# Strassen–Winograd down projection of a hybrid diffusion layer: its block products in another order, the last one's resident blocks loaded during the four products ahead of it, and the final norm by half rows

## The chip, the cores and the metric

The kernel runs on one core of one Trainium2 chip. The metric is the device time of one execution of the whole layer in microseconds (us), the median of several runs. Nothing is shared with other cores; all waits are between the engines of this core (TensorE, VectorE, ScalarE, GpSimd, and SyncE, which here only issues DMAs) and its DMA queues.

## The reference, cut to what matters

One layer over 1024 tokens of width D = 1024: a mixer (delta-rule and state-space heads) with a gated residual, then a gated MLP with a depthwise 3x3 convolution, another gated residual and a final RMS norm. The change lies in the last two lines only:

```python
def conv_glu(h, w_gate, w_up, conv_w, conv_b, w_down, on_grid):
    a = h @ w_gate
    ...
    return (jax.nn.silu(a) * (h @ w_up)) @ w_down
...
        x = x + g2 * conv_glu(modulate(rmsnorm(x, norm2_g[l]), sh2, sc2), *ffn_params, True)
        ...
    return rmsnorm(x, final_norm_g)
```

with `w_down` 2816 x 1024 (D_FF = 2816) and `rmsnorm(x, g) = x * rsqrt(mean(x*x) + EPS) * g`.

## The kernel before, in words

**The down projection as seven products.** The gated activations A (2816 features x 1024 tokens) and the weights B = `w_down` are cut into halves both ways, and the product is made by Winograd's form of Strassen's scheme with seven products instead of eight: P1 = A11·B11, P2 = A12·B21, P3 = S4·B22, P4 = A22·T4, P5 = S1·T1, P6 = S2·T2, P7 = S3·T3. The S are sums of quarters of A, the T of quarters of B. While gate and up are computed, GpSimd's queue writes all of A's seven operands to DRAM (`sa_d`) and the four T (`sw_d`); B11, B21 and B22 are read from `w_down` itself.

**One product.** The shared dimension is 1408 = NP x 128 with NP = 11, so a product is 11 blocks. A block has a stationary side (128 features x 512 tokens) and a moving side (128 features x 512 columns). `block()` fetches each side: a DMA of SyncE's queue into a raw buffer (`ra` or `rb`, two buffers each, L1418), a cast to fp32r on ScalarE (`sh`, `vh`: the high part, L1419) and a subtraction on VectorE (`sl`, `vl`: what the cast lost; it is issued through the helper of L95). These four have three buffers each, handed out by `parts()`. `mul()` (L1433) then runs three matmuls for one of the four token tiles of 128: high x high, high x low, low x high. A block is thus 12 matmuls on four PSUM banks, one bank a token tile, and a product 132. `accA` and `accB` are two sets of four banks; two successive products use different sets, so that the sums of one can be read while the next one runs.

**What is made of the products.** With s1 = P1, s2 = P1 + P6 and s3 = s2 + P7 (SBUF tiles `sn0`, `sn1`, `sn2` of four token tiles each), the four quarters of the result are P1 + P2 (token tiles 0 to 3, low columns `LOH`), s2 + P5 + P3 (tiles 0 to 3, high columns `HIH`), s3 + P5 (tiles 4 to 7, `HIH`) and s3 - P4 (tiles 4 to 7, `LOH`). `put(t, q, src)` multiplies a 128 x 512 piece by the gate row `g2row` into a temporary (`tm`, three buffers) and adds it to `x1[t]`, the residual stream of tile t in SBUF (`x_0` to `x_7` in the listings): two VectorE instructions. `put` is linear, so a quarter may be put in pieces: s2 + P5 and P3 are put one after the other.

**The order before** is P1 P6 P2 P7 P5 P4 P3. The last product has its first HEAD = 3 blocks like all others; the other eight (NLC = 8) are loaded into the space of the MLP's input `mxs`, which is free by then (`mxh`, `mxl`: high and low parts). They are called the resident blocks. With all of them in SBUF the matmuls can be run token tile by token tile instead of block by block. `final()` is the RMS norm of a whole row: ScalarE squares with a running sum, VectorE scales, GpSimd takes the power -1/2 (L1289), and one VectorE instruction (`stt`, L107) multiplies by that and by the gain row into `ot`, from where two DMAs write the row's halves, one issued by SyncE, one by ScalarE. For the very last tile the squares and the last multiply go by halves.

**What sets the order of the instructions.** The code is written product by product, but a scheduler orders the instructions of all engines by its own times ahead of the run, within their dependences. Each engine and each DMA queue then works through its list in order: what stands at the head and waits holds up all that is behind it. So the code's order is not the order on the engines, and the listings below are of the latter.

Of the kernel before, what the change touches and what calls it, by code (L numbers as in the profile page):

```python
# [13 lines left out]
ALU = mybir.AluOpType  # L14
# [59 lines left out]
def hybrid_layer(ctx: ExitStack, tc: tile.TileContext, x, c, cx, c_ctx, w_ada, b_ada, norm1_g, w_in,  # L74
# [13 lines left out]
    def T(pool, shape, name, dt=F32, **kw):  # L88
        return pool.tile(list(shape), dt, name=name, **kw)
# [1307 lines left out]
    accA = accB = None  # L1397


    PRODS = ("P1", "P6", "P2", "P7", "P5", "P4", "P3")  # L1400
    STA = dict(P1=0, P2=1, P4=2, P3=3, P5=4, P6=5, P7=6)
    MOV = dict(P5=0, P6=1, P7=2, P4=3)
    WD = dict(P1=(0, 0), P2=(1, 0), P3=(1, 1))
# [25 lines left out]
    def mul(pb, t, ops, start, stop):  # L1429
        (sh, sl), (vh, vl) = ops  # L1430
        tk = slice(t * P, (t + 1) * P)
        for n, (a, w) in enumerate(((sh, vh), (sh, vl), (sl, vh))):
            nc.tensor.matmul(pb, a[:, tk], w, start=start and n == 0, stop=stop and n == 2)  # L1433

    def product(p, acc, js, first, last):
        for j in js:
            ops = block(p, j, *parts())
            for t in range(4):
                mul(acc[t], t, ops, first and j == js[0], last and j == js[-1])

    with pool("fp") as fp:
        for n_, b_ in (("wr", 3), ("wh", 3), ("wl", 3)):
# [95 lines left out]
    with pool("p3") as p3:  # L1538
        s1, s2, s3 = (T(p3, [P, 4, 512], f"sn{i}") for i in range(3))
        g2 = rows[3]  # L1540
        accB = [bank(b) for b in ("A", "B", "E", "tp")]
        LOH, HIH = slice(0, 512), slice(512, D)

        def tmp_():
            cnt[0] += 1
            return T(p3, [P, 512], f"tm{cnt[0]}", tag="tm", bufs=3)

        def put(t, q, src):
            m = tmp_()
# [4 lines left out]
        def final(t, last):
            if "f" not in rows:
                rows["f"] = T(p3, [P, D], "gfrow")
                nc.sync.dma_start(rows["f"], final_norm_g.partition_broadcast(P))
            jk = T(p3, [P, D], f"fj{t}", tag="fj", bufs=2)
            ot = T(p3, [P, D], f"ot{t}", tag="ot", bufs=3)
            halves = [slice(0, 512), slice(512, D)]  # L1560
            if not last:
                rs = rstd_tok(x1[t], jk, t, 1)
                stt(ot, x1[t], rs, rows["f"], ALU.mult, ALU.mult)
            else:
                rs, a = ss2[:, 1, t:t + 1], ss2[:, 0, 0:2]
                for c, q in enumerate(halves):
                    act(jk[:, q], x1[t][:, q], AF.Square, accum_out=a[:, c:c + 1])
                tt(rs, a[:, 0:1], a[:, 1:2], ALU.add)
                ts(rs, rs, 1.0 / D, ALU.mult, EPS, ALU.add)
                nc.gpsimd.tensor_tensor(rs, rs, mhalf[:, 0:1], op=ALU.pow)  # L1570
            for c, q in enumerate(halves):
                if last:
                    stt(ot[:, q], x1[t][:, q], rs, rows["f"][:, q], ALU.mult, ALU.mult)
                (nc.scalar if c else nc.sync).dma_start(out[t * P:(t + 1) * P, q], ot[:, q])

        allj = range(NP)
        product("P6", accB, range(NP - 1), True, False)
        product("P1", accA, [NP - 1], False, True)
        for t in range(4):
            nc.scalar.copy(s1[:, t, :], accA[t])  # L1580
        product("P6", accB, [NP - 1], False, True)
        for t in range(4):
            tt(s2[:, t, :], accB[t], s1[:, t, :], ALU.add)
        product("P2", accA, allj, True, True)
        for t in range(4):
            m = tmp_()
# [20 lines left out]
        ops = []
        for u in range(NLC):
            sta, mov = ([m[:, u, 4 * i:4 * i + 4, :].rearrange("p k c -> p (k c)") for m in mxs] for i in range(2))
            ops.append(block("P3", HEAD + u, sta, mov))  # L1610
# [38 lines left out]
```

## Time and profile before

| | |
|---|---|
| median of 3 runs | 1557.68 us (1556.49 to 1559.80) |
| profiled execution | 1551.18 us |
| its span, first to last instruction | 1549.5 us |
| TensorE busy | 1450.4 us, 94% |
| VectorE busy | 1099.1 us, 71% |
| ScalarE busy | 694.1 us, 45% |
| GpSimd busy | 513.9 us, 33% |
| granted TensorE clock, mean | 0.974 |
| DMA traffic | 266.72 MB, 172 GB/s over the span |

The profile is of one execution, which is why it has a time of its own; its span leaves out what lies before the first and behind the last instruction. Times in it are us from the start of the span. Where an instruction is listed with its start, the next figure is its duration, then come engine, line, operation, output<-inputs and shape, and in square brackets how long its engine had been idle before and what ended that. The line of most VectorE instructions is that of a helper (L95 for a two-tensor operation, L102 for one with constants, L107 for a three-operand one), and L92 is ScalarE's, so that the tiles' names tell them apart. The seven products take up the last 245 us or so of the span.

### The profile page before, as it was taken

What the parts mean: (1) busy time and instruction counts of PE and PEld (TensorE: products, weight loads), DVE (VectorE), ACT (ScalarE), POOL (GpSimd) and SP (SyncE); (2) the same over time, 40 slices, a digit from 0 to 9 for tenths busy, and PEclk for the clock granted to TensorE, in tenths of its full rate; (3) what the DMA queues carried; (4) which work ended last, traced back from release to release, by engine and by line L of the source; (5) the groups of instructions that cost most, each with busy time, mean ns of one, the idle gap of its engine ahead of it and who ended that gap; (6) DMA issues with size and microseconds to landing.
All of it is one profiled execution on the core that took longest, in us unless ns stands there. A gap on an engine that the chain in (4) does not pass through costs nothing.

```text
span 1549.5 us, 23952 instructions
## 1 busy us (share of the span) xinstructions
PE 1450.4 (94%) x8344; PEld 1211.5 (78%) x8344; DVE 1099.1 (71%) x1749; ACT 694.1 (45%) x1552; POOL 513.9 (33%) x645
## 2 busy tenths in 40 slices
PE   5899988899999899998989799999999999999996
PEld 2577767778888789997767688888888888888885
DVE  6877688978535666547976887777778776456597
ACT  6566655636666656454243422222222221344444
POOL 3654499782226785201472111101111111000002
PEclk9999999999999999999999899999999999999998
DMA  8354877654668675535851434334444432566665
GB/s 279 120 160 136 234 224 215 166 149 120 177 192 292 207 263 168 150 117 179 291 169 69 149 120 146 125 133 156 143 149 156 144 140 105 180 198 194 191 188 192
DMA packets 255416, 266.72 MB, mean 172 GB/s; under 512 B 50657, under 2 KB 193630, under 8 KB 255296
## 3 DMA queue, kind: packets, MB, share of 16 engines
q1 hardware_dynamic: 238815, 212.90, 45.1%
q0 software_dynamic: 15136, 49.55, 8.4%
q10 hardware_dynamic: 1344, 2.75, 0.5%
q8 instruction: 66, 1.08, 0.3%
q14 instruction: 55, 0.44, 0.1%
HBM read 191.87 MB, written 73.27 MB: 171 GB/s over the span
## 4 chain that ended last, share of the span: by engine, by line
PE 60%; DVE 10%; DMA 8%; POOL 7%; issue 6%; ACT 2%; SPq 1%; POOLq 0%; DVEq 0%; ACTq 0%
PE bk L1298 29%; PE bk L1433 10%; PE bk L619 6%; PE bk L453 5%; POOL Zs L98 2%; POOL pr L98 2%; DMA rb<-rows_d 1%; PE bk L1346 1%; DMA owr<-in_w_out_dram 1%; DVE rs L107 1%; DVE fac L107 1%; DMA R<-rows_d 1%; PE bk L997 1%; DVE owl L95 1%; PE bk L1005 1%
## 5 line engine op out<-in xcount | busy, mean ns | idle before, releaser
L1298 PE MATMUL bk<-mxh,fh 128*128 128x512 f32 x672 | 262.5, 391 | 8.4 <-DVE fac L95 8.4
L1298 PE MATMUL bk<-mxl,fh 128*128 128x512 f32 x672 | 262.5, 391 | 0.0
L1298 PE MATMUL bk<-mxh,fl 128*128 128x512 f32 x672 | 262.0, 391 | 0.2 <-DVE fl L95 0.2
L107 DVE SCALAR_TENSOR_TENSOR fac<-gpad,v,fac 128x1024 f32<-128x1024 f32 x176 | 224.9, 1281 | 4.9 <-ACT fac L92 2.0
L1298 PEld LDWEIGHTS bk<-mxh,fh 128*128 128x128 f32 x672 | 126.8, 189 | 35.0 <-DVE fac L95 8.8
L1298 PEld LDWEIGHTS bk<-mxh,fl 128*128 128x128 f32 x672 | 126.7, 189 | 27.2 <-DVE fl L95 0.7
L1298 PEld LDWEIGHTS bk<-mxl,fh 128*128 128x128 f32 x672 | 126.7, 189 | 26.3
L1456 ACT CAST fh<-fr 128x1024 fp32r<-128x1024 f32 x42 | 44.3, 1055 | 228.9 <-PE bk L1298 215.6
L1520 POOL DMA_DIRECT2D sa_d<-fac x44 | 23.7, 540 | 352.0 <-issue 214.1
L453 PE MATMUL bk<-hh,wh 128*128 128x512 f32 x320 | 129.6, 406 | 0.8 <-DVE v L254 0.7
L453 PE MATMUL bk<-hh,wl 128*128 128x512 f32 x320 | 129.1, 403 | 0.0
L453 PE MATMUL bk<-hl,wh 128*128 128x512 f32 x320 | 128.1, 400 | 0.0
L95 DVE TENSOR_TENSOR fl<-fr,fh 128x1024 fp32r<-128x1024 f32 x42 | 51.3, 1221 | 101.6 <-ACT fh L1456 91.5
L1433 PE MATMUL bk<-vl,sh 128*128 128x512 f32 x276 | 107.5, 389 | 0.0
L1433 PE MATMUL bk<-vh,sl 128*128 128x512 f32 x276 | 107.4, 389 | 0.0
L1419 ACT CAST sh<-ra 128x512 fp32r<-128x512 f32 x69 | 43.0, 624 | 119.5 <-PE bk L1433 99.1
L95 DVE TENSOR_TENSOR sl<-ra,sh 128x512 fp32r<-128x512 f32 x69 | 47.5, 689 | 63.8 <-ACT sh L1419 63.8
L1289 POOL TENSOR_TENSOR ss<-ss,mhalf 128x1 f32<-128x1 f32 x15 | 13.9, 931 | 221.9 <-DVE ss L104 221.9
L1433 PE MATMUL bk<-vh,sh 128*128 128x512 f32 x276 | 75.7, 389 | 0.0
L453 PEld LDWEIGHTS bk<-hh,wh 128*128 128x128 f32 x320 | 61.7, 193 | 13.5 <-PE bk L252 0.9
L453 PEld LDWEIGHTS bk<-hh,wl 128*128 128x128 f32 x320 | 61.4, 192 | 13.1 <-issue 0.9
L453 PEld LDWEIGHTS bk<-hl,wh 128*128 128x128 f32 x320 | 61.7, 193 | 11.9 <-DVE hl L95 0.2
(386 smaller groups left out, 3730.7 us busy)
## 6 DMA issues: line engine op xcount, KB each, us to landing
ra<-sa_d SPq DMA_DIRECT2D x77, 256.0 KB
kv<-kv_d SPq DMA_DIRECT2D x80, 192.0 KB
yq<-yq_d SPq DMA_DIRECT2D x64, 192.0 KB
awa<-in_w_ada_dram SPq DMA_DIRECT2D x24, 512.0 KB
fr<-in_ffn_w_up_dram SPq DMA_DIRECT2D x22, 512.0 KB
dr<-in_ffn_w_down_dram SPq DMA_DIRECT2D x22, 512.0 KB
sa_d<-fac POOLq DMA_DIRECT2D x44, 256.0 KB, 2.3
rb<-sw_d SPq DMA_DIRECT2D x44, 256.0 KB
```

The lines of the kernel that those rows point to most:

```text
L95: nc.vector.tensor_tensor(o, a, b, op=op)
L98: nc.gpsimd.tensor_tensor(o, a, b, op=op)
L107: nc.vector.scalar_tensor_tensor(o, a, s, b, op0=op0, op1=op1)
L453: paced(nc.tensor.matmul(pb[:, :bn], w[i][:, kk, :], hview(h, k, b0, bn), start=(n == 0), stop=(n == 3 * KT - 1)))
L619: mm = nc.tensor.matmul(pb[:, 256 * j:256 * j + 256], m[:, k, tk], w, start=(n == 0), stop=(n == 3 * KT - 1))
L997: mm = nc.tensor.matmul(hi[d], yq[:, 0, :], r, start=True, stop=True)
L1005: mm = nc.tensor.matmul(lo[d], kd, ns[d], start=True, stop=True)
L1298: nc.tensor.matmul(pv, w(k), h[:, b4, k, :], start=(n == 0), stop=(n == 3 * KT - 1))
L1419: nc.scalar.copy(th, raw)
L1433: nc.tensor.matmul(pb, a[:, tk], w, start=start and n == 0, stop=stop and n == 2)
L1456: hi["last"] = nc.scalar.copy(wh, raw)
L1520: nc.gpsimd.dma_start(sa_d[i][j], t)
```

## The change

The order of the products becomes P1 P6 P7 P5 P4 P3 P2. What goes with it:

- **The last product is P2.** Its eight resident blocks are no longer loaded behind its own first three, but one by one through a hook that `product()` calls behind a block (`ahead`): one in P7, two in P5, three in P4, two in P3. They stay in `mxs` until the end.
- **The pieces are put at other times.** P1's part of the low columns of tiles 0 to 3 goes in on its own, in the code behind P7 (on VectorE the scheduler places it behind the end of P6), and P2's part at the end. s2 + P5 is put behind P4 in the code instead of behind P5.
- **The final norm goes by half rows.** The gain row is fetched before the first of the last products and scaled by sqrt(D) on ScalarE. `half1` handles the half of a row that is complete first: square with its sum on ScalarE, D·EPS added to the sum, the half multiplied by the gain in place. `half2` handles the other half: square, sum of the two halves' sums, power on GpSimd, the last multiply of this half on VectorE and of the other half on ScalarE (a copy with a scale). Both halves are written to the output from `x1` itself (L1580 by SyncE, L1581 by ScalarE); the tiles `ot` are gone. Before, this was for the last tile only, and both multiplies were VectorE's.

The number of products, blocks and matmuls is as before. The core of the diff:

```diff
-    PRODS = ("P1", "P6", "P2", "P7", "P5", "P4", "P3")
+    PRODS = ("P1", "P6", "P7", "P5", "P4", "P3", "P2")
...
-    def product(p, acc, js, first, last):
+    def product(p, acc, js, first, last, between=None):
         for j in js:
             ops = block(p, j, *parts())
             for t in range(4):
                 mul(acc[t], t, ops, first and j == js[0], last and j == js[-1])
+            if between is not None:
+                between(j)
...
+        gf = rows["f"] = T(p3, [P, D], "gfrow")
+        nc.sync.dma_start(gf, final_norm_g.partition_broadcast(P))
+        nc.scalar.mul(gf, gf, float(D) ** 0.5)
+        sq = T(p3, [P, 2, NLC], "sq")
...
+        def half1(t, q, c):
...
+            square(t, 0, q)
+            ts(sq[:, 0, t:t + 1], sq[:, 0, t:t + 1], D * EPS, ALU.add)
+            tt(x1[t][:, q], x1[t][:, q], gf[:, q], ALU.mult)
+
+        def half2(t, q, c):
+            square(t, 1, q)
+            rs = ss2[:, 1, t:t + 1]
+            tt(rs, sq[:, 0, t:t + 1], sq[:, 1, t:t + 1], ALU.add)
+            nc.gpsimd.tensor_tensor(rs, rs, mhalf[:, 0:1], op=ALU.pow)
+            o = HIH if q is LOH else LOH
+            stt(x1[t][:, q], x1[t][:, q], rs, gf[:, q], ALU.mult, ALU.mult)
+            act(x1[t][:, o], x1[t][:, o], AF.Copy, scale=rs)
+            nc.sync.dma_start(out[t * P:(t + 1) * P, q], x1[t][:, q])
+            nc.scalar.dma_start(out[t * P:(t + 1) * P, o], x1[t][:, o])
...
+        def ahead(at):
+            def f(j):
+                if j in at:
...
+                    rest.append(block("P2", HEAD + u, sta, mov))
+            return f
...
-        product("P2", accA, allj, True, True)
+        product("P7", accA, allj, True, True, ahead((8,)))
+        for t in range(4):
+            tt(s3[:, t, :], accA[t], s2[:, t, :], ALU.add)
+        for t in range(4):
+            put(t, LOH, s1[:, t, :])
+        product("P5", accB, allj, True, True, ahead((5, 8)))
         for t in range(4):
             m = tmp_()
-            tt(m, accA[t], s1[:, t, :], ALU.add)
-            put(t, LOH, m)
...
+            tt(m, accB[t], s3[:, t, :], ALU.add)
+            tt(s2[:, t, :], accB[t], s2[:, t, :], ALU.add)
+            put(4 + t, HIH, m)
+            half1(4 + t, HIH, 1)
+        product("P4", accA, allj, True, True, ahead((4, 6, 8)))
         for t in range(4):
-            tt(s3[:, t, :], accB[t], s2[:, t, :], ALU.add)
-        product("P5", accA, allj, True, True)
+            put(t, HIH, s2[:, t, :])
         for t in range(4):
             m = tmp_()
-            tt(m, accA[t], s3[:, t, :], ALU.add)
-            tt(s2[:, t, :], accA[t], s2[:, t, :], ALU.add)
-            put(4 + t, HIH, m)
-            put(t, HIH, s2[:, t, :])
-        product("P4", accB, allj, True, True)
+            tt(m, s3[:, t, :], accA[t], ALU.subtract)
+            put(4 + t, LOH, m)
+            half2(4 + t, LOH, 0)
+        product("P3", accB, allj, True, True, ahead((5, 8)))
+        product("P2", accA, range(HEAD), True, False)
         for t in range(4):
-            m = tmp_()
-            tt(m, s3[:, t, :], accB[t], ALU.subtract)
-            put(4 + t, LOH, m)
-            final(4 + t, False)
-        HEAD = NP - NLC
-        product("P3", accA, range(HEAD), True, False)
...
+            put(t, HIH, accB[t])
+            half1(t, HIH, 1)
         for t in range(4):
             for u in range(NLC):
-                mul(accA[t], t, ops[u], False, u == NLC - 1)
-            put(t, HIH, accA[t])
-            final(t, t == 3)
+                mul(accA[t], t, rest[u], False, u == NLC - 1)
+            put(t, LOH, accA[t])
+            half2(t, LOH, 0)
```

Three places in the engines' lists show what the scheduler makes of it.

First, TensorE at the start of the resident blocks of the last product. `bk_12786` to `bk_12789` are the banks of token tiles 0 to 3. Before:

```order
L1433 MATMUL bk_12786<-mxh 128x512
L1433 MATMUL bk_12787<-mxh 128x512
L1433 MATMUL bk_12788<-mxh 128x512
L1433 MATMUL bk_12789<-mxh 128x512
L1433 MATMUL bk_12786<-mxl,mxh 128x512
L1433 MATMUL bk_12786<-mxh,mxl 128x512
L1433 MATMUL bk_12787<-mxl,mxh 128x512
L1433 MATMUL bk_12787<-mxh,mxl 128x512
```

and now:

```order
L1433 MATMUL bk_12786<-mxh 128x512
L1433 MATMUL bk_12786<-mxl,mxh 128x512
L1433 MATMUL bk_12786<-mxh,mxl 128x512
L1433 MATMUL bk_12786<-mxh 128x512
L1433 MATMUL bk_12786<-mxl,mxh 128x512
L1433 MATMUL bk_12786<-mxh,mxl 128x512
```

Before, the scheduler put the four tiles side by side, block by block, although the code is written tile by tile, and the tiles end together. Now the list goes tile by tile, 24 matmuls each.

Second, VectorE in P4, from the last split of block 6 (the subtraction that makes its `vl`) to that of block 7. `sn_13035` is s2, `sn_13036` is s3, and the first `vl` and the last are block 6's and block 7's. Before:

```order
L95 TENSOR_TENSOR vl_14336<-rb_14341,vh_14335 128x512
L95 TENSOR_TENSOR x_6_8733<-x_6_8733,tm_14174 128x512
L95 TENSOR_TENSOR tm_14180<-bk_12789,sn_13036 128x512
L95 TENSOR_TENSOR sn_13035<-bk_12789,sn_13035 128x512
L95 TENSOR_TENSOR x_2_8729<-x_2_8729,tm_14177 128x512
L95 TENSOR_TENSOR sl_14358<-ra_14361,sh_14357 128x512
L95 TENSOR_TENSOR vl_14360<-rb_14365,vh_14359 128x512
```

and now:

```order
L95 TENSOR_TENSOR vl_14104<-rb_14109,vh_14103 128x512
L95 TENSOR_TENSOR x_0_8727<-x_0_8727,tm_14237 128x512
L95 TENSOR_TENSOR tm_14243<-sn_13035,g2row 128x512
L102 TENSOR_SCALAR sq<-sq 128x1
L95 TENSOR_TENSOR x_7_8734<-x_7_8734,gfrow 128x512
L95 TENSOR_TENSOR x_1_8728<-x_1_8728,tm_14240 128x512
L95 TENSOR_TENSOR mxl<-ra_14125,mxh 128x512
L95 TENSOR_TENSOR mxl<-rb_14129,mxh 128x512
L95 TENSOR_TENSOR tm_14246<-sn_13035,g2row 128x512
L95 TENSOR_TENSOR sl_14134<-ra_14137,sh_14133 128x512
L95 TENSOR_TENSOR x_2_8729<-x_2_8729,tm_14243 128x512
L95 TENSOR_TENSOR vl_14136<-rb_14141,vh_14135 128x512
```

Between the two there were five instructions and are now ten. Counted from the first sum that reads P5's banks (`tm<-bk,sn`, at the end of P5), block 7's last split was the 32nd instruction and is the 47th, 43 of them 128 x 512 and 4 of one column. The 15 that have come in ahead of it are the splits of two resident blocks (four, `mxl`), four multiplies by the gain row (`gfrow`), the four of one column (`sq`), and three of the updates of `x_7` and `x_3`. The puts of s2 into `x_0` to `x_3` stand in P4 in both lists, although the code now has them behind P4.

Third, SyncE's queue in P3. `x_4` to `x_7` are output rows, `sa_d_105` is S4, P3's stationary operand, and `sa_d_103` is A12, that of a resident block of P2. Before, at the same place in the list, when the resident blocks of P3 were loaded:

```order
L1574 DMA out_dram<-ot_14461 128x512
L1418 DMA ra_14611<-sa_d_105 128x512
L1418 DMA rb_14615<-in_ffn_w_down_dram 128x512
L1418 DMA ra_14619<-sa_d_105 128x512
L1418 DMA rb_14623<-in_ffn_w_down_dram 128x512
L1574 DMA out_dram<-ot_14474 128x512
```

and now:

```order
L1580 DMA out_dram<-x_4_8731 128x512
L1418 DMA ra_14445<-sa_d_103 128x512
L1418 DMA rb_14449<-in_ffn_w_down_dram 128x512
L1418 DMA ra_14457<-sa_d_105 128x512
L1418 DMA rb_14461<-in_ffn_w_down_dram 128x512
L1580 DMA out_dram<-x_5_8732 128x512
```

In both lists the writes of the finished rows stand among the loads, and a write waits at the head of the queue until its row is ready. Before, the loads behind them were those of resident blocks 5 to 8 of the last product; now they are those of a resident block and of P3's own blocks 6 to 9.

More of the change, by code (lines that the diff above doesn't have):

```diff
@@ L1551, in put @@
             tt(x1[t][:, q], x1[t][:, q], m, ALU.add)
[L1554 to L1574, printed above, removed]
@@ new lines, in hybrid_layer, with square @@
+        gf = rows["f"] = T(p3, [P, D], "gfrow")
+        nc.sync.dma_start(gf, final_norm_g.partition_broadcast(P))
+        nc.scalar.mul(gf, gf, float(D) ** 0.5)
+        sq = T(p3, [P, 2, NLC], "sq")
+        def square(t, c, q):
+            cnt[0] += 1
+            jk = T(p3, [P, 512], f"fj{cnt[0]}", tag="fj", bufs=2)
+            act(jk, x1[t][:, q], AF.Square, accum_out=sq[:, c, t:t + 1])
+        def half1(t, q, c):
+            square(t, 0, q)
+            ts(sq[:, 0, t:t + 1], sq[:, 0, t:t + 1], D * EPS, ALU.add)
+            tt(x1[t][:, q], x1[t][:, q], gf[:, q], ALU.mult)
@@ L1576, in hybrid_layer @@
+        HEAD = NP - NLC
+        rest = []
+        def ahead(at):
+            def f(j):
+                if j in at:
+                    u = len(rest)
+                    sta, mov = ([m[:, u, 4 * i:4 * i + 4, :].rearrange("p k c -> p (k c)") for m in mxs]
+                                for i in range(2))
+                    rest.append(block("P2", HEAD + u, sta, mov))
+            return f
         allj = range(NP)
@@ L1589, in hybrid_layer @@
-        product("P7", accB, allj, True, True)
+            tt(m, accB[t], s3[:, t, :], ALU.add)
[3 more added lines that the diff above has]
+        product("P4", accA, allj, True, True, ahead((4, 6, 8)))
         for t in range(4):
-            tt(s3[:, t, :], accB[t], s2[:, t, :], ALU.add)
-        product("P5", accA, allj, True, True)
+            put(t, HIH, s2[:, t, :])
         for t in range(4):
             m = tmp_()
-            tt(m, accA[t], s3[:, t, :], ALU.add)
-            tt(s2[:, t, :], accA[t], s2[:, t, :], ALU.add)
-            put(4 + t, HIH, m)
-            put(t, HIH, s2[:, t, :])
@@ L1599, in hybrid_layer @@
-        product("P4", accB, allj, True, True)
-        for t in range(4):
-            m = tmp_()
-            tt(m, s3[:, t, :], accB[t], ALU.subtract)
-            put(4 + t, LOH, m)
-            final(4 + t, False)
-        HEAD = NP - NLC
-        product("P3", accA, range(HEAD), True, False)
[L1607 to L1610, printed above, removed]
+            tt(m, s3[:, t, :], accA[t], ALU.subtract)
```

## The prediction

> **What bounds the kernel now.** I read the page's head, then the busy time by stretches over the down projection, then TensorE's waits there, the chain that ended last, and the timelines of TensorE, VectorE, ScalarE and the SyncE queue. The stretches first (us, then busy us and instruction count of each engine, the granted TensorE clock, the DMA share):
>
> ```profile
> span 1549.5 us, 23952 instructions
> ...
> core 0: us, PE busy (x) PEld busy (x) DVE busy (x) ACT busy (x) POOL busy (x), PEclk, DMA share, GB/s
> 1400.00:1475.00 75.00, 75.00 (x332) 62.13 (x331) 45.95 (x74) 31.10 (x55) 0.00 (x0) 1.00 0.63 192
> 1475.00:1505.00 30.00, 30.00 (x134) 24.83 (x133) 27.17 (x45) 13.45 (x23) 0.00 (x0) 1.00 0.59 183
> 1505.00:1535.00 30.00, 29.67 (x131) 24.27 (x130) 24.20 (x41) 15.02 (x26) 6.13 (x4) 1.00 0.69 219
> 1535.00:1549.50 14.50, 0.65 (x3) 0.19 (x1) 9.70 (x18) 4.67 (x10) 3.51 (x4) 0.60 0.37 145
> ```
>
> TensorE never rests until 1535, then 14 us follow without it. But in 1475 to 1505, which is P4, VectorE is busy for 27.17 of 30 us: a second engine stands close to its limit there. Two lines of the waits since 1300 (who waited for whom, us in total, times, longest), and three pieces of the chain:
>
> ```profile
> ACT sh L1419 <- PE bk L1433: 99.1, 54, 19.4
> ...
> PE bk L1433 <- DVE mxl L95: 0.3, 1, 0.3
> ```
> ```profile
> 1326.27 151.56 PE bk L1433 x669
> ...
> 1477.83 0.58 DVE x L95
> ...
> 1522.10 5.50 DMA ra<-sa_d
> ```
>
> ScalarE's casts wait 99 us for TensorE to give a buffer back, so loads mostly lie ready; TensorE itself has one visible wait. The chain is TensorE's until 1477.8 and then runs through VectorE and the loads. A matmul takes 151.56/669 = 0.2265 us, a block (12) 2.72, a product (132) 29.9. The end of TensorE's timeline:
>
> ```profile
> 1529.42 1.07 PE L1433 MATMUL bk<-mxh 128*128 128x512 f32 x4
> 1530.82 0.50 PE L1433 MATMUL bk<-mxl,mxh 128*128 128x512 f32 x1 [0.33 <-DVE mxl L95]
> ...
> 1535.26 0.39 PE L1433 MATMUL bk<-mxh,mxl 128*128 128x512 f32 x1
> ```
>
> From 1529.42 to 1535.26 start 24 matmuls, 23 steps of 0.2265 = 5.21 us; they took 5.84, so that wait cost 0.63. The last matmul ends at 1535.65, so **the tail is 13.85 us**. All four tiles finish together and queue in it.
>
> **The tail.** What a single tile's chain costs stands in these rows of VectorE, ScalarE and GpSimd:
>
> ```profile
> 1414.30 0.68 DVE L95 TENSOR_TENSOR tm<-bk,sn 128x512 f32<-128x512 f32 x1
> 1415.02 0.69 DVE L95 TENSOR_TENSOR tm<-tm,g2row 128x512 f32<-128x512 f32 x1
> ...
> 1542.17 0.15 DVE L95 TENSOR_TENSOR ss<-ss 128x1 f32<-128x1 f32 x1
> ...
> 1544.70 1.41 DVE L107 SCALAR_TENSOR_TENSOR ot<-x,ss,gfrow 128x512 f32<-128x512 f32 x2 [0.66 <-POOL ss L1570]
> ```
> ```profile
> 1536.30 1.06 ACT L92 ACTIVATE fj<-x 128x1024 f32<-128x1024 f32 x1 [5.08 <-DVE x L95]
> ...
> 1539.76 0.61 ACT L92 ACTIVATE fj<-x 128x512 f32<-128x512 f32 x1
> 1540.28 0.19 ACT L92 ACTIVATION_READ_ACCUMULATOR fj<-x 128x1 f32 x1
> ```
> ```profile
> 1511.28 2.75 POOL L1289 TENSOR_TENSOR ss<-ss,mhalf 128x1 f32<-128x1 f32 x1 [180.79 <-DVE ss L104]
> 1517.28 0.93 POOL L1289 TENSOR_TENSOR ss<-ss,mhalf 128x1 f32<-128x1 f32 x1 [3.26 <-DVE ss L104]
> ...
> 1544.12 0.55 POOL L1570 TENSOR_TENSOR ss<-ss,mhalf 128x1 f32<-128x1 f32 x1 [1.46 <-DVE ss L104]
> ```
>
> Before, VectorE ends at 1544.70 + 1.41 = 1546.11, and 3.39 us go to the last write and the end. After, tiles 0 to 2 finish under TensorE (a tile's 24 matmuls are 5.4 us, its chain 4), so behind the last matmul stands one tile: multiply 0.72 (a dependent step, 1414.30 to 1415.02), add 0.68, square and its read 0.71, one-column add 0.15, power 0.74 (between 0.55 and 0.93), last multiply 0.71 (half of 1.41), and five handovers of 0.03 (1544.67 to 1544.70) to 0.1, 0.3 together: 4.0. ScalarE's scaled copy of the other half runs beside that last multiply. With 3.39 the tail is 7.4, **6.45 less**. The 0.63 goes too, as the resident blocks lie ready: **7.1 gained**, 6.6 if the chain is half a us longer.
>
> **What the change loads onto P4.** P4's first matmul is 263 steps before the last: 1535.26 - 0.63 - 263 x 0.2265 = 1475.06. Block b's splits are due 2.72b later; its first four matmuls read the casts alone, which gives 0.91 more. VectorE before:
>
> ```profile
> 1474.14 0.68 DVE L95 TENSOR_TENSOR tm<-bk,sn 128x512 f32<-128x512 f32 x1
> ...
> 1492.78 0.68 DVE L95 TENSOR_TENSOR vl<-rb,vh 128x512 fp32r<-128x512 f32 x1
> ...
> 1497.60 0.68 DVE L95 TENSOR_TENSOR vl<-rb,vh 128x512 fp32r<-128x512 f32 x1
> ```
>
> The epilogue of P5 begins at 1474.14, 0.92 ahead. To 1497.60 stand 40 instructions without a gap: 23.46/39 = 0.6015 apiece. Block 7's last split is the 32nd and ends at 1493.46, 18.4 after P4's start; due at 19.0 + 0.91 = 19.9. VectorE is 1.5 early, so no wait shows.
>
> After, by the order, it is the 47th: 43 large ones and 4 of one column (0.15 busy, half of it overlapped: 0.3 together). It ends at -0.92 + 43 x 0.6015 + 0.3 + 0.08 = 25.3, **5.4 late**. What stands ahead of it now: the splits of two resident blocks (4), four multiplies by the gain row, four of one column, and three instructions of the updates that before came behind block 7. VectorE works in order, so the loads wait. SyncE waits too: with two raw buffers a load may only issue when the split two loads back is done.
>
> ```profile
> 1480.86 0.32 SPq L1418 DMA_DIRECT2D ra<-sa_d  x1
> ...
> 1522.10 0.32 SPq L1418 DMA_DIRECT2D ra<-sa_d  x1
> ```
> ```profile
> 1483.47 0.62 ACT L1419 CAST sh<-ra 128x512 fp32r<-128x512 f32 x1 [1.89 <-DMA ra<-sa_d]
> ...
> 1527.62 0.62 ACT L1419 CAST mxh<-ra 128x512 fp32r<-128x512 f32 x1 [3.32 <-DMA ra<-sa_d]
> ```
>
> Issue to cast took 2.61 us. With 0.62 for the cast, 0.68 for the split and about 0.2 of handovers a buffer turns in 4.1, so a load may come every 2.05; P4's 14 loads in 29.9 us need 2.14. Nothing is left to catch up with: 0 to 2 more, taken at 1.0. **P4: +6.4**, from 5.0 to 7.4.
>
> **P3.** Two resident blocks and the epilogue with the norm of tiles 4 to 7. Up to block 6's last split stand 27 large instructions and 4 small ones, and the first power takes 2.75 (row above), of which 1.1 is not covered. From -0.92 that is 16.9, due 17.2: nothing lost. But the lag out of P4 lets VectorE begin only at about +0.8, and the cast of block 6 stands on ScalarE behind a square that waits for tile 7: up to 2.6 late. Then four output writes stand among the loads in SyncE's queue. Each waits for VectorE's last multiply of its tile; behind the first stand the loads of a resident block and of block 6, for which VectorE and TensorE wait. With such writes under way a load before took 5.50 instead of 2.61 (1522.10 to 1527.62): up to 4 more, if three loads are 2.9 late and the two buffers take them in pairs. **P3: +2.9**, from 0 to 6.6; nearer to 2.6, since P4 is sure to hand over a lag.
>
> [...]
>
> **The rest.** At P6's end the update with P1 alone puts 5 more large instructions ahead of P7's second block; its margin by the same count is 0.5, at block 2 0.2: 0 to +0.5, taken at 0.3. The gain row is now scaled on ScalarE during P1 (1.06 for 128x1024 by the first row of ScalarE above), hidden since the casts there wait for TensorE's buffers; without that cover it costs its 1.06. Four more large VectorE instructions (P1's share added on its own) are in the counts above. P7 and P5 have room: 30 instructions x 0.6015 are 18 of 29.9 us. Below zero nothing can go but the tail: TensorE runs the same 924 matmuls.
>
> **Sum**: -7.1 + 6.4 + 2.9 + 0.3 = +2.5 on the profiled execution's 1551.18 (1.7 above its span). The median of the runs is 1557.68; the difference carries over: **1560.2**. Ends: -7.1 + 5.0 = -2.1 and -6.6 + 7.4 + 6.6 + 0.5 = +7.9. The measurement can tell about 0.2%, 3.1 us, from no change.
>
> **Rivals.**
> 1. *The cover holds.* Two blocks split ahead hide the longer queue. For it: before, P4 ran with no wait at 27.17 of 30. Against: 43 instructions would have to take 0.48 apiece, and every one of 40 took 0.60. It gives -7.1 + 0 to 2, about 1551.6. Chance 0.15.
> 2. *Only P4 lags*, by 6.1, and P3 catches up: -0.7, 1557.0. For it: the count from -0.92. Chance 0.15.
> 3. *Loads behind output writes in P3* (the slower side). Three loads at 5.50 instead of 2.61 are 8.7 late, half of which reaches the splits: P3 costs 2.6 + 4.0 = 6.6 and the whole is -7.1 + 6.4 + 6.6 + 0.3 = +6.2, 1563.9. It decides when a load beside a write takes over 3.1 us: a buffer then turns in 4.6, 2.3 a load, and 13 loads fill P3's 29.9. Against: only one such row. Chance 0.17.
> 4. *The clock drops in the waits.* Behind the last matmul the granted clock falls:
>
> ```profile
> 1537.00:1538.00 1.00, 0.00 (x0) 0.00 (x0) 1.00 (x3) 0.95 (x3) 0.00 (x0) 0.95 0.00 0
> 1538.00:1539.00 1.00, 0.00 (x0) 0.00 (x0) 1.00 (x4) 0.95 (x3) 0.25 (x1) 0.50 0.00 0
> ```
>
> that is 2.3 us after 1535.65. My longest single wait is 2.6. Two drops of ten matmuls each at half rate cost 4.6 more: 1564.8. Chance 0.05. [...]
>
> That the last product isn't run tile by tile is excluded by the order of TensorE.
>
> **Chances.** The forecast has 0.48. Its own range is 1558.5 to 1564; I put 0.30 of it within 3.1 us and 0.18 above. Faster: rival 1, 0.15. Same: 0.30 + 0.15 = 0.45. Slower: 0.18 + 0.17 + 0.05 = 0.40. The range, from the sum's lower end to its upper one with half a us on each side for the median, is 1555 to 1566; it leaves out rival 1 and the far end of 3 and 4.
>
> **What will show it.** Right: TensorE waits for VectorE's vl in P4's blocks 5 to 7, 5 to 7 us in all, and in P3 around block 6; the tail behind the last matmul is 7 to 8 us; no wait for mxl at the end. Wrong: no wait in P4 (the count fails), a tail above 9 (the chain), waits of P3 above 6 with late loads (rival 3), a granted clock of 0.5 within P4 or P3 (rival 4).

## The result, and the profile after

The changed kernel takes **1567.26 us** (median of 8 runs, 1561.94 to 1572.82), the kernel before 1557.24 (8 runs, 1552.00 to 1561.22). The ratio is 1.0070, 95% interval 1.0054 to 1.0086: 8 to 13 us slower, where 2.5 slower was forecast with a range that ended at 1566.

The profiled execution shows where. The busy time by stretches over the last part of the changed kernel, columns as before:

```profile
span 1563.2 us, 23980 instructions
```
```profile
1445.00:1475.00 30.00, 26.55 (x108) 20.60 (x106) 26.95 (x49) 15.57 (x29) 0.00 (x0) 0.94 0.56 170
1475.00:1505.00 30.00, 28.42 (x116) 22.59 (x117) 24.19 (x42) 15.56 (x30) 3.08 (x2) 0.94 0.69 215
1505.00:1535.00 30.00, 26.65 (x109) 21.24 (x108) 22.75 (x42) 16.76 (x33) 1.48 (x2) 0.94 0.63 207
1535.00:1563.20 28.20, 20.36 (x90) 16.52 (x88) 9.18 (x16) 5.79 (x12) 2.20 (x4) 0.94 0.20 75
```

TensorE, which before had one wait of 0.33 us ahead of the end, now has holes in P4 and P3, and the granted clock is 0.94 where it was 1.00. The waits of TensorE in the last part, and P4's and P3's on its timeline:

```profile
PE bk L1433 <- ACT vh L1419: 5.4, 4, 2.3
PE bk L1433 <- DVE vl L95: 2.9, 2, 1.5
```
```profile
1465.39 1.21 PE L1433 MATMUL bk<-vh,sh 128*128 128x512 f32 x4 [1.34 <-ACT vh L1419]
1468.02 0.80 PE L1433 MATMUL bk<-vl,sh 128*128 128x512 f32 x1 [1.42 <-DVE vl L95]
...
1475.06 1.20 PE L1433 MATMUL bk<-vh,sh 128*128 128x512 f32 x4 [0.75 <-ACT vh L1419]
1477.78 0.64 PE L1433 MATMUL bk<-vl,sh 128*128 128x512 f32 x1 [1.52 <-DVE vl L95]
...
1508.55 0.68 PE L1433 MATMUL bk<-vh,sh 128*128 128x512 f32 x1 [2.29 <-ACT vh L1419]
...
1519.68 0.50 PE L1433 MATMUL bk<-vh,sh 128*128 128x512 f32 x1 [1.06 <-ACT vh L1419]
```

The first two pairs are blocks 5 and 7 of P4, the last two rows blocks 6 and 9 of P3. Summing the steps between matmuls beyond 0.2265 us, P4 loses 9.6 and P3 5.6 us (such sums are good to about 0.2); some of that is the clock. The tail is the forecast one: the last of all matmuls starts at 1554.97 and ends at 1555.36, and 7.84 us follow (13.85 before).

From here on **the projection** means the time from the first matmul of P1 to the end of the span, since what lies ahead is the same code in all kernels and varies from execution to execution: that first matmul starts at 1303.7 in the profile before, 1308.6 in the one after, and between 1303.5 and 1314.6 in those of the experiments. The projection took 245.8 before and takes 254.6: +8.7, within the interval of the medians.

### The profile page after: what moved, and what is told of

The parts are those of the page before. It is cut to its first block, busy times and chain, and to the rows that moved or that the text cites. A ratio compares the mean times of both kernels' runs of the same rounds, so it can differ in the third digit from the quotient of the medians.

```text
span 1563.2 us, 23980 instructions
## 1 busy us (share of the span) xinstructions
PE 1461.3 (93%) x8344; PEld 1213.5 (78%) x8344; DVE 1100.7 (70%) x1767; ACT 706.0 (45%) x1575; POOL 512.2 (33%) x645
## 4 chain that ended last, share of the span: by engine, by line
PE 58%; DVE 11%; DMA 9%; POOL 6%; issue 6%; ACT 2%; SPq 1%; POOLq 0%; DVEq 0%; ACTq 0%
PE bk L1298 28%; PE bk L1433 10%; PE bk L453 5%; PE bk L619 5%; POOL Zs L98 2%; POOL pr L98 1%; DMA awa<-in_w_ada_dram 1%; DMA R<-rows_d 1%; DMA owr<-in_w_out_dram 1%; DMA ra<-sa_d 1%; DVE owl L95 1%; DVE fac L107 1%; DMA rb<-rows_d 1%; DVE rs L107 1%; PE bk L997 1%
## 5 line engine op out<-in xcount | busy, mean ns | idle before, releaser
L1576 POOL TENSOR_TENSOR ss<-ss,mhalf 128x1 f32<-128x1 f32 x8 | 6.8, 845 | 216.2 <-DVE ss L95 216.2
```

## Experiments

Each kernel is the changed one with the edit shown. "Lost" is TensorE's time beyond 0.2265 us a matmul, from its timeline. The times are medians of 4 to 12 runs, and each ratio is to runs of the kernel before that were taken along with them (medians 1555.80 to 1557.24). The other columns are from the one profiled execution.

| run | time, us | ratio to before, 95% interval | projection | lost in P4 | in P3 | elsewhere | tail |
|---|---|---|---|---|---|---|---|
| before | 1557.24 | | 245.8 | 0 | 0.6 (its last product) | 0 | 13.85 |
| after | 1567.26 | 1.0070 (1.0054 to 1.0086) | 254.6 | 9.6 | 5.6 | 0 | 7.84 |
| e1_early | 1562.11 | 1.0039 (1.0023 to 1.0054) | 249.7 | 2.6 | 0 | 7.6 | 7.82 |
| e2_late | 1554.58 | 0.9984 (0.9968 to 1.0000) | 243.1 | 0.6 | 0.5 | 0.6 | 9.82 |
| e3_fold | 1565.80 | 1.0059 (1.0036 to 1.0082) | 251.7 | 6.3 | 6.1 | 0 | 7.82 |
| e4_fill | 1567.10 | 1.0060 (1.0041 to 1.0080) | 256.2 | 7.1 + 3.6 filled | 2.6 + 3.6 filled | 0 | 7.79 |
| e5_early_own | 1552.78 | 0.9989 (0.9976 to 1.0003) | 241.7 | 0.6 | 1.2 | 0.5 | 7.81 |
| e6_own | 1552.88 | 0.9981 (0.9967 to 0.9994) | 240.9 | 0.8 | 0.7 | 0 | 7.81 |
| e7_early_fold_own | 1549.03 | 0.9962 (0.9944 to 0.9980) | 239.1 | 0 | 0 | 0 | 7.77 |
| e8_late_fold | 1555.48 | 0.9998 (0.9983 to 1.0012) | 242.6 | 0 | 0.4 | 0.4 | 10.30 |
| e9_held | 1571.76 | 1.0097 (1.0079 to 1.0115) | 258.0 | 12.6 | 6.2 | 0 | 7.84 |
| e10_split_gp | 1572.19 | 1.0099 (1.0078 to 1.0120) | 261.2 | 13.1 | 8.6 | 0.4 | 7.82 |
| e11_p5clear | 1564.38 | 1.0045 (1.0029 to 1.0062) | 254.4 | 8.2 | 6.9 | 0 | 7.82 |
| e12_held_act | 1562.26 | 1.0035 (1.0019 to 1.0050) | 250.6 | 4.1 | 7.4 | 0 | 7.83 |

### Resident loads elsewhere: e1_early, e2_late

```diff
-        product("P6", accB, range(NP - 1), True, False)
+        product("P6", accB, range(NP - 1), True, False, ahead((3, 6)))
...
-        product("P7", accA, allj, True, True, ahead((8,)))
+        product("P7", accA, allj, True, True, ahead((3, 5, 8)))
...
-        product("P5", accB, allj, True, True, ahead((5, 8)))
+        product("P5", accB, allj, True, True, ahead((2, 4, 6)))
...
-        product("P4", accA, allj, True, True, ahead((4, 6, 8)))
+        product("P4", accA, allj, True, True)
...
-        product("P3", accB, allj, True, True, ahead((5, 8)))
+        product("P3", accB, allj, True, True)
```

> The changed kernel with its eight resident loads moved out of P4 and P3: two in P6, three in P7, three in P5. VectorE's list in P4 up to block 7's last split falls from 47 to 36 instructions (33 large): 33 x 0.6015 + 0.3 = 20.1 from the epilogue's first sum. Theory (VectorE's list in P4 makes TensorE wait, each wait is followed by 3.4 us at half clock): P4's loss goes from 9.6 us to 0 to 0.5, no half clock in P4, P3's loss goes from 5.6 to 0 to 4 as nothing is handed over; from the first matmul of the projection to the end 241 to 246 us instead of 254.6; time 1553 to 1558. Rival (the loads themselves, two raw buffers and shared DMA engines, set the pace): the waits move with the loads to P6, P7 and P5, the projection stays at 251 to 256 us and the time at 1563 to 1568.

Neither: 249.7 us. P4's loss falls to 2.6 and no stretch at half clock is left, as the theory has it, but P7 and P5 now lose 6.8, as the rival has it (0.8 more lie in P2). The waits in P7 and P5, and three of the 31 loads of stationary sides in SyncE's queue there, the first, the ninth and the last:

```profile
DVE sl L95 <- ACT sh L1419: 14.6, 16, 1.5
ACT sh L1419 <- DMA ra<-sa_d: 14.4, 14, 1.9
...
PE bk L1433 <- ACT vh L1419: 4.7, 7, 1.0
```
```profile
1375.18 0.32 SPq L1418 DMA_DIRECT2D ra<-sa_d  x1
...
1398.08 0.32 SPq L1418 DMA_DIRECT2D ra<-sa_d  x1
...
1448.04 0.32 SPq L1418 DMA_DIRECT2D ra<-sa_d  x1
```

Here VectorE waits for casts and ScalarE for loads. The loads go out every (1448.04 - 1375.18)/30 = 2.43 us, but that takes in the stretch from 1384 to 1397, where the sums at P6's end keep VectorE busy for 11.80 of 13 us and splits come late: the buffer whose load was issued at 1386.91 was free only 9.3 us later. From 1398.08 on nobody but the loads is late, and they go out every (1448.04 - 1398.08)/22 = 2.27 us, while 14 in a product need 2.14. So in this place the pace of the loads limits, at 2.27 and not at the 2.05 of the prediction.

The second run puts the resident loads back behind P2's third block:

```diff
         product("P2", accA, range(HEAD), True, False)
+        for j in range(NLC):
+            ahead((j,))(j)
```

(and no `ahead` in the products before).

> The changed kernel with the eight resident loads back where the kernel before had them, all behind P2's third block; products' order, puts and norm by halves stay. VectorE's list in P4 is the same as with the loads moved early. Theory: P4's loss 0 to 0.5, P3's 0 to 4, and the end falls back to tiles side by side: tail 12 to 14 us instead of 7.8, a wait of 0.6 to 3 at the resident blocks; the projection takes 246 to 251 us. Rival (order of products or puts is at fault, not the loads ahead): P4 and P3 lose 10 us or more all the same, the projection takes 256 us or more.

243.1 us, below what was expected: P4 loses 0.6, P3 0.5, and the tail is 9.8, not 12. The new order of the products and the halved norm are thus not what costs: without loads ahead the new order is 2.7 us shorter than the old one in the profile, and the interval of the ratio ends at 1.0000.

### VectorE's list: e3_fold, e8_late_fold

```diff
-        for t in range(4):
-            put(t, HIH, s2[:, t, :])
...
-            put(t, HIH, accB[t])
+            m = tmp_()
+            tt(m, accB[t], s2[:, t, :], ALU.add)
+            put(t, HIH, m)
             half1(t, HIH, 1)
```

> The changed kernel with s2 + P5 put together with P3 behind P3 (sum first, one put) instead of on its own: eight VectorE instructions leave P4, four come into P2's head. The list up to block 7's last split falls from 47 to 40 (36 large), resident loads stay in P4. Theory: block 7's split comes 7 x 0.6 = 4.2 us earlier, so P4 loses about 4 instead of 9.6 (3.6 late plus at most one slow stretch), P3's loss is 2 to 5.6; the projection takes 246 to 250 us, time 1558 to 1563. Rival (the loads set the pace): the loads come as late as before, P4's loss stays above 8, the projection at 252 or more.

251.7 us, between the two. P4 loses 6.3 instead of 9.6, a gain of 3.3 where 5.6 was expected, and P3 6.1, no less than before. The shorter list helps, but not by all of its length: the loads at P5's end are still late, and the epilogue begins 0.6 behind P4's first matmul (1.5 in the changed kernel) instead of 0.9 ahead.

> The new order with the resident loads behind P2's third block and s2 + P5 put together with P3: no loads ahead. The same without the joint put took 243.1 us with 0.6 of loss in P4 and 0.5 in P3. VectorE theory: both small losses go, projection 241.5 to 243 us, time 1553 to 1555; if the list in P4 had no part, no difference to 243.1 within 0.5.

242.6 us, tail 10.3: the losses in P4 are gone, but the profile's 0.5 against the same kernel without the edit can't be told from none in the times.

### The clock: e4_fill

Eight matmuls into a bank that is free, on the block before (the scheduler placed those for P4's block 7 in block 6, those for P3's blocks 6 and 9 in its blocks 4 and 8):

```diff
         for j in js:
+            if (p, j) in FILL:
+                fill(acc, prev)
...
+    FILL = (("P4", 5), ("P4", 7), ("P3", 6), ("P3", 9))
```

> The changed kernel with eight extra matmuls (8 x 0.2265 = 1.8 us, results overwritten) ahead of blocks 5 and 7 of P4 and blocks 6 and 9 of P3, where TensorE waits: it works in the time in which it stood idle. Theory (the half clock follows from TensorE's idle time in the 3.4 us before): no stretch at half clock is left, or at most one; VectorE still sets when block 7 can go on, so P4 saves only the slow steps behind block 7, about 1.9, and P3 about 1.7, less up to 0.8 for the needless part at block 9: the projection takes 250 to 253 us instead of 254.6. Rival (the clock drops from something else, as load on the other engines or DMA): three slow stretches of 3.4 us stay, and the extra matmuls cost up to 3 more: 255 to 258.

Of three stretches at half clock one is left, at another place (the three columns behind the busy times are the clock, the DMA share and GB/s):

```profile
1489.00:1490.00 1.00, 1.00 (x5) 0.80 (x4) 0.39 (x1) 0.00 (x0) 0.00 (x0) 0.77 1.00 377
1490.00:1491.00 1.00, 1.00 (x4) 0.77 (x3) 0.13 (x1) 0.76 (x2) 0.00 (x0) 0.50 0.94 182
```

But the projection is not shorter, 256.2: the 7.25 us of filling took the place of 5.5 us of loss. In P4 the time that was gained behind block 7 came back as a wait of 1.87 for block 9's cast. The halved clock is real, but without it P4 waited for the next block's load instead. How much of P3's it cost stays open, since the filling itself costs at block 9.

### Raw buffers: e5_early_own, e6_own, e7_early_fold_own

The resident loads get raw buffers of their own, two per side, in the space that is free by then:

```diff
-    def block(p, j, sta, mov):
+    def block(p, j, sta, mov, own=None):
...
-            raw = T(p2, [P, 512], f"{'rb' if which else 'ra'}{cnt[0]}", tag="rb" if which else "ra", bufs=2)
+            rn = ("q" if own else "r") + "ab"[which]
+            raw = T(own or p2, [P, 512], f"{rn}{cnt[0]}", tag=rn, bufs=2)
...
-                    rest.append(block("P2", HEAD + u, sta, mov))
+                    rest.append(block("P2", HEAD + u, sta, mov, p3))
```

> The resident loads early (two in P6, three in P7, three in P5), and now through raw buffers of their own (two per side) in the same SyncE queue. With them early and sharing the raw buffers the projection took 249.7 us from its first matmul to the end, with 6.8 us of waits in P7 and P5 for casts of late loads (2.43 us a load where 14 a product need 2.14) and 2.6 in P4. Theory A (a raw buffer's turn, load 3.2 + cast 0.6 + split 0.7 + handovers, limits the loads): P7 and P5 lose 0 to 1.5, P4 0 to 1.5; projection 241 to 245 us, time 1552 to 1556. Theory B (the DMA engines or SyncE's in-order queue limit): waits of 5 us or more stay in P7 and P5, projection 248 to 251.

241.7 us against 249.7 with shared buffers, and nothing of note lost in P7 and P5: the numbers of theory A.

> The changed kernel as it is, resident loads in P7, P5, P4 and P3, but through raw buffers of their own. Theory A (raw buffers' turn makes P4 start 2.4 us late and keeps loads from catching up; VectorE's list of 47 adds 5.4): P4's loss 5 to 7 instead of 9.6, P3's 2 to 5 instead of 5.6, projection 247 to 251 instead of 254.6. Theory B (DMA engines): no change, 253.5 to 256. Theory C (raw buffers alone, VectorE's list matters little): P4's loss below 2, projection below 246.

240.9 us and 0.8 lost in P4, the numbers of theory C. But both runs changed more than the buffers. Free of the shared ones, the scheduler moved all eight resident loads to the end of P1 and the start of P6, in e5 as in e6 (in e6 their splits stand at 1353.6 to 1374.6, and P4 starts at 1456), and VectorE's list in P4 has 36 instructions up to block 7, as in e1. They don't tell the buffers from the list in P4; e9 to e12 try that.

What e6 does show is the buffers' part in the pace of the loads. The 30 us in which the resident loads go out, and the first and the last of the 20 loads of stationary sides (into `ra` and the new buffer) that SyncE issues around them:

```profile
1344.00:1374.00 30.00, 30.00 (x134) 24.84 (x133) 22.51 (x35) 22.45 (x37) 0.00 (x0) 1.00 0.97 340
```
```profile
1341.24 0.33 SPq L1419 DMA_DIRECT2D ra<-sa_d  x1
...
1373.73 0.32 SPq L1419 DMA_DIRECT2D ra<-sa_d  x1
```

That is 32.49/19 = 1.71 us a load, where e1 had 2.27, with TensorE busy throughout. The queue and the DMA engines (0.97 busy) can do it. Two raw buffers a side can't: the shortest turn of one in e1, from its load's issue to the end of its split, was 3.9 us, which makes 1.9 a load.

> Resident loads early with raw buffers of their own, and s2 + P5 put together with P3 (four VectorE instructions fewer, eight fewer in P4). If raw buffers and VectorE's list in P4 are the causes, nothing but P3's ScalarE list is left (0 to 2.5): projection 240 to 243 us (231.9 of matmuls with P1's interleaved start, 7.8 of tail, the rest waits), time 1551 to 1554, ratio to the kernel before 0.996 to 0.998. If the DMA engines limit, 247 or more.

No loss at all, 1549.03 us, 0.9962 of before: the best version, faster than both kernels. TensorE has no wait from P1 to the end, and VectorE keeps 4 us of slack in P4 (the second row):

```profile
1301.00:1445.00 144.00, 144.00 (x637) 119.29 (x636) 92.46 (x141) 65.14 (x109) 8.61 (x16) 1.00 0.66 218
1445.00:1475.00 30.00, 30.00 (x134) 24.86 (x133) 26.15 (x47) 15.82 (x30) 0.00 (x0) 1.00 0.63 191
1475.00:1505.00 30.00, 30.00 (x134) 24.82 (x134) 22.93 (x40) 17.41 (x33) 5.76 (x4) 1.00 0.76 249
1505.00:1534.50 29.50, 29.50 (x132) 24.39 (x130) 18.79 (x35) 9.10 (x20) 1.65 (x3) 1.00 0.14 55
```

### List or buffers: e9_held, e10_split_gp, e11_p5clear, e12_held_act

Own buffers, and a one-column write on GpSimd that holds each load in its place:

```diff
+            if own:
+                nc.gpsimd.tensor_tensor(raw[:, 0:1], cur[0][0][0][:, 0:1].bitcast(F32), mhalf[:, 0:1], op=ALU.mult)
```

> The changed kernel with raw buffers of their own for the resident loads, and each load held in its place by a one-column GpSimd write to the raw buffer that reads the block just cast: unlike in the run with own buffers alone, where the scheduler moved all resident loads ahead of P7's end, two resident blocks are split in P5, three in P4, two in P3, as in the changed kernel. In VectorE's list of P4 block 9's last split is the 53rd (49 large): -0.92 + 49 x 0.6015 + 0.3 + 0.1 = 28.9 after P4's start, due 24.5 + 0.9. Theory V (VectorE's list): P4 loses 3 to 5 us, the projection takes 243 to 247. Theory A (the shared raw buffers alone): P4 and P3 lose under 1.5 each, as with the loads moved, the projection takes 240 to 242.

Slower than all theories: the hold made a wait of its own. GpSimd's one-column writes, and SyncE's queue beside one of them:

```profile
1460.82 0.19 POOL L1413 TENSOR_TENSOR qb<-sh,mhalf 128x1 f32<-128x1 f32 x1
1468.16 3.20 POOL L1413 TENSOR_TENSOR qa<-sh,mhalf 128x1 f32<-128x1 f32 x1 [7.15 <-ACT sh L1422]
...
1478.20 4.61 POOL L1413 TENSOR_TENSOR qa<-sh,mhalf 128x1 f32<-128x1 f32 x1 [6.69 <-ACT sh L1422]
```
```profile
1464.06 0.32 SPq L1421 DMA_DIRECT2D rb<-sw_d  x1
1471.39 0.32 SPq L1421 DMA_DIRECT2D qa<-sa_d  x1
```

For 7.3 us the queue stood behind one resident load, and the blocks' loads behind it. The run says nothing on list or buffers.

Splitting the resident blocks on GpSimd, buffers shared:

```diff
-            tt(tl, raw, th.bitcast(F32), ALU.subtract)
+            (ptt if own else tt)(tl, raw, th.bitcast(F32), ALU.subtract)
```

> The changed kernel with the subtractions of the resident blocks (16 in all, 6 in P4) on GpSimd instead of VectorE; raw buffers stay shared. VectorE's list in P4 loses the resident splits, but the loads of the blocks now come later in the list (block 7's last split is the 44th, 40 large: 23.5 after the start if that is on time, 3.6 late). Theory V: P4 loses 3 to 6 instead of 9.6, the projection takes 248 to 252. Theory A: a raw buffer is given back no earlier, P5 still ends with late loads and P4 starts late by 2 or more, the projection stays at 253 to 257.

261.2 us, P4 loses 13.1: worse than either theory. Its splits took 1.29 us at the median, but 2.77 and 3.88 for two of those in P4, and the raw buffers were held for that long. Taking work off VectorE did not help where it lengthened a buffer's turn.

P5's two resident loads moved to P6, all else left, VectorE's list in P4 word for word that of the changed kernel:

```diff
-        product("P6", accB, range(NP - 1), True, False)
+        product("P6", accB, range(NP - 1), True, False, ahead((3, 6)))
...
-        product("P5", accB, allj, True, True, ahead((5, 8)))
+        product("P5", accB, allj, True, True)
```

> The changed kernel with P5's two resident loads in P6 instead; P4's three and P3's two stay, raw buffers shared, VectorE's list in P4 word for word the same (block 7's last split the 47th). Theory V: P4 starts without the lag of 2.4 that P5's late loads gave it, its splits are 25.3 after the start, 5.4 late: P4 loses 5 to 7.5 instead of 9.6, P3 3 to 5.6, the projection takes 249 to 252.5. Theory A (loads through shared raw buffers in P4 itself): P4 loses 8 or more as before, the projection 253 or more. If the lag alone was the cause, P4 loses under 3 and the projection is below 247.

P4's first matmul is at 1449.21, and the rows of VectorE are the epilogue's first sum and block 7's last split:

```profile
1448.33 0.69 DVE L95 TENSOR_TENSOR tm<-bk,sn 128x512 f32<-128x512 f32 x1
...
1473.83 0.68 DVE L95 TENSOR_TENSOR vl<-rb,vh 128x512 fp32r<-128x512 f32 x1
```

The sum begins 0.88 before P4's start, and the split ends 25.3 behind it: the count of the prediction to a tenth. P4 loses 5.4 up to there, as theory V has it, but 2.8 more behind it, mostly at half clock (matmul steps of 0.43 us instead of 0.2265), so that its 8.2 and the 254.4 of the whole are theory A's numbers. The lag out of P5 is worth 1.4 in P4, and P3 gives it back (6.9).

Last, the held loads again, held by a one-column copy on ScalarE:

```diff
+            if own:
+                act(raw[:, 0:1], cur[0][0][0][:, 0:1].bitcast(F32), AF.Copy)
```

> As the held loads, but the hold is a one-column copy on ScalarE instead of GpSimd (in the run before, GpSimd's one-column writes took 3.2 and 4.6 us while VectorE was busy without a gap, and the loads behind them in SyncE's queue waited: a new wait of its own). Raw buffers of their own; two resident blocks are split in P5, three in P4, two in P3, as in the changed kernel. VectorE's list in P4: block 9's last split is the 53rd, 28.9 after the start, due at 25.4. Theory V (VectorE's list makes P4 wait): P5 ends on time, P4 loses 3 to 6 with VectorE busy throughout, the projection takes 243 to 249. Theory A (sharing the raw buffers is all): P4 and P3 lose under 1.5 each, projection 240 to 242. If SyncE's queue is held up again, waits for casts of 2 us or more with VectorE idle.

P4 (its stretch, its waits and block 9's last split below) loses 4.1, with VectorE busy for all 30.00 of 30 us and the clock at 1.00. Block 9's last split ends at 1481.96, 29.3 behind P4's first matmul (1452.70) where 28.9 was expected; it was due at 25.4, and the 3.9 that it is late are P4's loss. VectorE's list makes P4 wait without any help of shared buffers, theory V.

```profile
1453.00:1483.00 30.00, 26.69 (x116) 21.20 (x115) 30.00 (x54) 17.91 (x39) 0.00 (x0) 1.00 0.66 201
```
```profile
PE bk L1436 <- DVE vl L95: 3.3, 2, 1.8
```
```profile
1481.28 0.68 DVE L95 TENSOR_TENSOR vl<-rb,vh 128x512 fp32r<-128x512 f32 x1
```

P3, however, loses 7.4, and the projection is longer than theory V had it. Its own loads now run beside two resident ones and the output writes; one load and its cast:

```profile
1509.20 0.38 SPq L1421 DMA_DIRECT2D rb<-in_ffn_w_down_dram  x1
```
```profile
1516.14 0.62 ACT L1422 CAST vh<-rb 128x512 fp32r<-128x512 f32 x1 [3.97 <-DMA rb<-in_ffn_w_down_dram]
```

The cast comes 6.9 us behind the issue, and ScalarE stood idle for the last 3.97 of them. Loads beside output writes are what rival 3 describes, but two resident loads were issued just ahead as well (1508.16 and 1508.78), and the run doesn't tell which of the two made this load late. In the changed kernel itself the slowest loads of P3 took 4.65 and 4.36 us from issue to cast, and the one wait of TensorE there that a late load may have made is the 1.06 at block 9.

## Why the prediction was wrong

The direction was right, the size was not: +8.7 in the profile against +2.5, and the time beyond the range's end. By the steps of the prediction:

- **The tail and the wait at the resident blocks: right.** Forecast -6.45 and -0.63, measured -6.0 and -0.6. TensorE runs tile by tile, and one tile's chain is left.
- **P4: the mechanism right, the size too small, 6.4 against 9.6.** The count of VectorE's list (25.3 behind P4's start) was exact where P5 ends in time (e11), and e12 shows the list alone. What failed is a sentence elsewhere, which put P5's part at nothing: "P7 and P5 have room: 30 instructions x 0.6015 are 18 of 29.9 us". It looked at VectorE only, which was indeed busy for 18.69 of the 30 us from 1420. But P5 has 13 loads, one in 2.30 us, and a load comes every 2.27 us, not 2.05 (e1); in the changed kernel's own P5 they went out every (1447.80 - 1423.61)/11 = 2.20, and a pair near the end took 4.33 from issue to cast. So the loads just kept up, and that slow pair made them late. At P5's end ScalarE waited for one of them, VectorE sat idle for its cast, and the epilogue began 1.5 us behind P4's first matmul (1450.07) instead of 0.9 ahead:

```profile
1449.00 0.62 ACT L1419 CAST vh<-rb 128x512 fp32r<-128x512 f32 x1 [2.49 <-DMA rb<-sw_d]
```
```profile
1449.65 0.69 DVE L95 TENSOR_TENSOR vl<-rb,vh 128x512 fp32r<-128x512 f32 x1 [2.42 <-ACT vh L1419]
...
1451.54 0.68 DVE L95 TENSOR_TENSOR tm<-bk,sn 128x512 f32<-128x512 f32 x1
...
1477.04 0.69 DVE L95 TENSOR_TENSOR vl<-rb,vh 128x512 fp32r<-128x512 f32 x1
```

  Block 7's split ends at 1477.73, 27.7 behind the start, 2.4 more than forecast: 7.7 late instead of 5.4. TensorE's losses up to there add up to that 7.7, the first slow stretch among them. The other 1.9 come behind it, 1.6 of them at half clock.
- **The turn of a raw buffer: the mis-sized term.** 4.1 was put together from one quick load (2.61 from issue to cast). At a load every 2.27 us a turn, with two buffers, is 4.5. From issue to cast 30 loads of e1 took 3.2 on average, and to the start of the split 4.1; the twelve of e6 into `ra`, with loads 1.71 apart, took 5.1 to the start of the split, in which VectorE's list may have a part. The longer turn is also behind the lag that was passed on into P3, where the epilogue begins 1.8 behind the first matmul.
- **P3: 2.9 forecast, 5.6 measured.** The cast of block 6 came up to 2.6 late behind the norm of tiles 6 and 7 on ScalarE, as written: 2.45 is lost there. ScalarE's order:

```profile
1506.13 0.62 ACT L1419 CAST sh<-ra 128x512 fp32r<-128x512 f32 x1
1506.66 0.72 ACT L92 ACTIVATE x<-x,ss 128x512 f32<-128x512 f32 x1
1507.28 0.61 ACT L92 ACTIVATE fj<-x 128x512 f32<-128x512 f32 x1
...
1507.89 0.60 ACT L1419 CAST vh<-rb 128x512 fp32r<-128x512 f32 x1
```

  The scaled copy that the change put there and a square stand between the two casts. 1.7 more went at half clock and 1.4 at block 9. In e7, with the same copies and squares on ScalarE, but loads in time and without the four casts of resident blocks there, P3 loses nothing: the copies and squares alone cost nothing.
- **Rival 4, the clock in the waits (0.05): it came, and was priced too low in chance.** Three stretches, 3.4 us each, at a granted clock of 0.50. The prediction measured it by the longest single wait, and none in the changed kernel exceeded 2.29; the falls came in or behind the second of two waits in P4 and behind one wait in P3, with TensorE busy for 35, 41 and 33% of the 3.41 us ahead (last section). In each stretch the matmuls took about 1.7 more, where 2.3 was priced; a drop of ten matmuls, as priced, no run shows: 3.4 us at the measured step of 0.43 hold eight. What that added to the time stays open: e4 took two of the three away and the time stayed, but with 7.25 us of filling in their place.
- **Rival 1, the cover holds: fell**, as it holds only without resident loads in P4 (e2, e6). **Rival 2, only P4 lags: fell**, P3 lost 5.6. **Rival 3**: loads in P3 did take over its 3.1 us (up to 4.65), but at most the 1.4 at block 9 is theirs; in e12 late loads decide, though not shown to be late through the writes. **P6 and P7 (+0.3): nothing lost there.**

So the loss has two causes that feed each other, loads of resident blocks that take turns with the blocks' own in two raw buffers, and their splits in a VectorE list that is already full in P4. Loads moved ahead through shared buffers (e1: 10.2 us), a shorter list alone (e3: 12.4) or own buffers with the loads held in place (e12: 11.5, most of it in P3) each leave a loss. Own buffers with the loads moved to P1 and P6 leave 2.3 and 1.5 (e5, e6), and with a shorter list as well nothing (e7). How P3's loss divides between the two causes, ScalarE's list and the clock stays open.

## What to carry to other kernels

A product that prefetches for a later one must be counted for every engine and buffer that the prefetch passes, in the product where it is issued and in the next, which inherits the lag; an engine with 40% idle time there (VectorE, busy for 18.69 of 30 us in P5) is no room if the buffers turn too slowly. Give prefetches buffers of their own: they no longer take turns with the loads that are needed next, and a scheduler is free to put them where there is slack. Where they stayed in the full products, own buffers were not enough (e12). And read a load's turn where the queue is busy, not from one that ran alone.

## What the runs showed of the hardware

- **The granted clock fell to 0.50 three times in P4 and P3, for 3.4 us each.** Rows of the changed kernel, one us each, PE clock third from the end:

```profile
1467.00:1468.00 1.00, 0.00 (x0) 0.00 (x0) 1.00 (x3) 0.96 (x2) 0.00 (x0) 0.87 0.67 217
...
1469.00:1470.00 1.00, 1.00 (x4) 0.76 (x3) 1.00 (x3) 0.72 (x2) 0.00 (x0) 0.50 0.97 344
...
1471.00:1472.00 1.00, 1.00 (x5) 0.78 (x5) 1.00 (x3) 0.45 (x1) 0.00 (x0) 0.92 0.66 219
```

  0.87 and 0.92 put the fall at 1467.74 and the rise at 1471.16, 3.4 us apart; in between a matmul step was 0.43 us instead of 0.2265. The two other falls, read in the same way in stretches of a tenth of a us, are at 1477.98 and 1508.70, that is 3 and 12 times 3.41 behind the first, and their rises at 1481.40 and 1512.11. In the 3.41 us ahead of each fall TensorE was busy for 35, 41 and 33%. That share alone does not settle it: in e3, after waits of 0.69 and 1.46 in block 5 of P4, it was 37% in the 3.41 us up to 1470.95, and the clock stayed at 1.00. It stayed at 1.00 in the changed kernel behind the wait of 1.06 at P3's block 9, too. What sets the falls is not shown.
- **A one-column GpSimd instruction took 0.19 us, or 3.20 and 4.61** (e9, rows above). Three rows of VectorE beside them:

```profile
1460.29 0.68 DVE L95 TENSOR_TENSOR tm<-bk,sn 128x512 f32<-128x512 f32 x1
...
1470.63 0.68 DVE L95 TENSOR_TENSOR vl<-rb,vh 128x512 fp32r<-128x512 f32 x1
...
1482.68 0.14 DVE L102 TENSOR_SCALAR sq<-sq 128x1 f32<-128x1 f32 x1
```

  The 0.19 (at 1460.82) passed beside sums that read one input from PSUM (`bk`), with VectorE as busy. All through the 3.20 (1468.16 to 1471.36) VectorE ran instructions with two SBUF inputs without a gap; the last of them ended at 1471.31, and VectorE paused. Beside the 4.61 (1478.20 to 1482.81) stood such instructions too, up to one of a single input (1482.68 to 1482.82). These are times that agree; that the one engine held up the other is not shown. In e10 two of GpSimd's splits in P4 took 2.77 and 3.88 where the median was 1.29; what made them long is not shown either.
